# A decoder layer on one core: a new order of the opening stage, with block sums behind the shifts and one fold of squares

## The chip, the cores and the metric

One core of a Trainium2 chip runs one program. The metric is device time in microseconds (us) of one execution; the kernel before takes 1634.56 us as the median of 3 runs (1634.46 to 1636.76). Engines: PE (TensorE, matrix products), DVE (VectorE), ACT (ScalarE), POOL (GpSimd), SP (SyncE, which issues the loads).

## What is computed

A layer of a decoder on x of 1024 tokens by 1024 channels, in f32. Cut to the part that the change touches:

```python
mod = silu(cond) @ w_mod + b_mod                    # shifts, scales and gates
(sh1, sc1, g1, sh2, sc2, g2, sh3, sc3, g3) = split(mod, 9)
h = rms_norm(x, ffn1_norm) * (1 + sc1) + sh1
x = x + 0.5 * g1 * ((silu(h @ w_gate) * (h @ w_up)) @ w_down)
```

Behind this come a mixing layer (a short convolution beside a diagonal state-space model), a second feed-forward layer of the same form, and a last norm.

## The kernel before, in words

Tokens lie along the free axis in two halves of 512 (h = 0 and 1), channels on the 128 partitions in 8 blocks (k = 0 to 7). PE multiplies f32 values as pairs of a rounded high part and a rest: `mm3` (L342) makes each product of 128 by 128 by 512 from three matmuls, high by high, high by low, low by high. So every weight tile needs a rounding on ACT (`Weights.cast`, L173) and a subtraction on DVE (L177), and every block of activations a rounding (L980) and a subtraction (L984).

The opening stage (L845 to L1034) runs from the start until the first 64 products of the feed-forward layer are done: 2 halves, 8 blocks, 4 weight tiles of 128 output columns. Its instructions on PE, DVE, ACT and SP are written out by hand: `STEPS` (L1014) is a list of words, each word calls a function `do_...` with its digits, and the block `manual_schedule` (L1026) keeps that order on each of the four engines. Each engine works through its own queue in order. Instructions from outside the list can be placed between them by the scheduler. The words:

- `warm7`: 7 fillers (L926), matmuls of a bf16 tile of ones with itself, 512 columns, whose result nobody reads.
- `silu`, `cps0`, `cps1`, `cact`: silu of cond on one row, spread to 128 partitions by an f32 matmul with one row of weights for each 512 columns (L914), copied to SBUF (L918).
- `sqa12`, `sqd12`: the squares of the load of x with half 1 and pair of blocks 2, on ACT (L933) or on DVE (L937). `add12` folds the two blocks of a pair into one on DVE (L942). `stp12` adds a pair into the sum over all channels (L948): one f32 matmul of 512 columns if the pair was folded, two if not.
- `ya1`, `y1`: from the sum of half 1 the inverse root on ACT (L959, L960), and one step that sharpens it on DVE (L963, L964).
- `mods1`: for block 1 the two dot products with silu(cond) on DVE (L524; scale first, shift second) and two small instructions (L971, L972). The new words `ma1` and `mb1` are its two parts.
- `sc10`, `hi10`, `lo10` for block 1, half 0: scale (DVE, L976), shift and round (ACT, L980), shift and rest (DVE, L984).
- `wh0`, `wl0`: the rounding and the rest of weight tile 0. Tile 4, for the next stage, waits for a buffer that comes free when the products of tile 0 are done.
- `p111`: the product of half 1, block 1, weight tile 1.
- `x11`, `cols`, `half10`, `load3`, `rawh0`, `raw2`: loads issued by SP: a quarter of a half of x (512 KB), the table of small vectors (64 KB), half of a modulation block (512 KB), a whole one (1 MB), half of the first raw weight block, a whole one. There are four buffers for modulation blocks, and raw blocks 2 and 3 go where raw blocks 0 and 1 lay.
- `Weights.combine` (L154), the block sums: three passes of DVE (L157 to L159) over raw weight block 3 for the products of the next stage. It is called by `pump` (L184) and lies outside the list before; the new word `cmb3` calls it from the list.

```python
for c in range(2 - ((h, j) in added)):
    T.matmul(st[h][:], lhsT=means[D][:].to_broadcast([P, P]), rhs=sq[h, j][:, c, :], ...)
```

Of the kernel before, what the change touches and what calls it, by code (L numbers as in the profile page):

```python
# [13 lines left out]
F32 = mybir.dt.float32  # L14
# [7 lines left out]
P = 128  # L22
# [197 lines left out]
def hymba_layer(ctx: ExitStack, tc, x_d, wm1_d, wmod_d, gu1_d, gg1_d, gs1_d, wd1_d, win_d, wout_d, glu_d, gu2_d, gs2_d, wd2_d, cols_d, cond_d, lam_d, bc_d, out_d):  # L220
    nc = tc.nc
    V, A, T, SP = nc.vector, nc.scalar, nc.tensor, nc.sync

    def pool(name, bufs=1, **kw):
        return ctx.enter_context(tc.tile_pool(name=name, bufs=bufs, **kw))
# [11 lines left out]
    cact = pool("cap").tile([P, 1024], F32, name="cact")  # L237
# [22 lines left out]
    def t2k(name):  # L260
        return tmp.tile([P, HALF], F32, tag="t", name=name)

    cols = const.tile([P, NCOLS], F32, name="cols")
# [7 lines left out]
    gains = const.tile([P, C_CW - C_N1], F32, name="gains")  # L271
# [55 lines left out]
    ws = Weights((V, A, SP), srcs, granules, 2)  # L327
# [5 lines left out]
    def x_tile(k, h, nm):  # L333

        xt[k][h] = mov(f"{nm}{k}_{h}", dtype=F32)
        for i in range(2):
            x[2 * k + i][h] = xt[k][h][:, i, :]
        return xt[k][h][:]
# [183 lines left out]
    def mod_vector(w, s):  # L522

        V.tensor_tensor_reduce(out=w, in0=w, in1=cact[:], scale=1.0, scalar=0.0, op0=ALU.mult, op1=ALU.add, accum_out=s)  # L524
# [316 lines left out]
    pro = pro_open.enter_context(tc.tile_pool(name="pro", bufs=1))  # L841
# [10 lines left out]
    mw = {}  # L852

    def halves(t):

        return t.rearrange("p a c -> (p a c)").rearrange("(a p c) -> a p c", a=2, p=P)

    def mod_load(k, half=None):
        if k not in mw:
            mw[k] = pro.tile([P, 2, 1024], F32, tag="mw", name=f"mw{k}", bufs=4)  # L860
        if half is None:
            SP.dma_start(mw[k][:], wm1_d[k])
        else:
            SP.dma_start(mw[k][:, half, :], halves(wm1_d[k])[half])

    def raw_load(half):
        if not raw0:
            raw0.append(ws.blank())
        SP.dma_start(raw0[0][:, half, :], halves(gu1_d[0])[half])

    def x_load(h, j):
        SP.dma_start(x_tile(j, h, "x"), x_d[h, j])

    raw0 = []
    raw_load(0)
    x_load(1, 0)
    x_load(1, 2)
    x_load(1, 3)
    mod_load(1, 0)
    x_load(1, 1)  # L880
    SP.dma_start(cols[:], cols_d)
    mod_load(1, 1)
    mod_load(0, 0)
    mod_load(0, 1)
    x_load(0, 3)
    x_load(0, 1)
    x_load(0, 2)
    x_load(0, 0)
    raw_load(1)
    ws.load(2)  # L890
    mod_load(5)
    mod_load(2)
    b1 = cols[:, C_BMOD + SC1 * KT : C_BMOD + (SC1 + 1) * KT]
    cps = [ps(f"cp{i}") for i in range(2)]
    bcs = [pro.tile([P, HALF], F32, name=f"pbc{h}") for h in range(2)]
# [67 lines left out]
        V.scalar_tensor_tensor(out=y2[h], in0=st[h][:], scalar=EPS, in1=y2[h], op0=ALU.add, op1=ALU.mult)  # L963
        V.scalar_tensor_tensor(out=bcs[h][:], in0=y2[h], scalar=-3.0, in1=y[h], op0=ALU.add, op1=ALU.mult)  # L964

    def do_mods(k):
        m = pro.tile([P, 2], F32, tag="m", name=f"m{k}", bufs=2)
        for c in range(2):
            mod_vector(mw[k][:, c, :], m[:, c : c + 1])
        gn, sh = gains[:, k : k + 1], cols[:, C_BMOD + SH1 * KT + k : C_BMOD + SH1 * KT + k + 1]  # L970
        V.scalar_tensor_tensor(out=scl[:, 0, k : k + 1], in0=m[:, 0:1], scalar=gn, in1=pre[:, k : k + 1], op0=ALU.mult, op1=ALU.add)  # L971
        V.tensor_tensor(out=mods[:, 0, k : k + 1], in0=m[:, 1:2], in1=sh, op=ALU.add)  # L972
# [20 lines left out]
    def do_p(h, k, i):  # L993
# [4 lines left out]
        if i == 0 and made[0, 0] == made[1, 0] == KT:  # L998
            ws.slots.append(ringp)
            ws.freed += 1  # L1000

    def do_half(k, c):
        mod_load(k, c)

# [7 lines left out]
        ws.load(i + 1)  # L1012

    STEPS = """  # L1014
    warm7 warm7 warm1 silu wh0 ars wl0 sqd12 sqa10 cps0 cps1 sqa13 add12 add10 stp12 cact add13 stp10 sqa11 stp13 gains add11 mods1
    load3 warm3 stp11 ya1 mods0 sqa03 y1 sqa01 add03 sqa02 add01 warm7 warm7 warm7 warm2 stp03 sc11 sqa00 stp01 add02 hi11 add00
    stp02 wh1 sc01 stp00 lo11 hi01 p110 wl1 raw2 load7 ya0 p111 lo01 wh2 p101 y0 p100 wh3 sc10 wl2 hi10 warm7 p112 lo10 p102 sc00
    p010 wl3 hi00 p011 p113 lo00 p001 mods5 load6 raw3 p000 p013 p003 p002 sc51 p103 sc50 hi51 p012 hi50 lo51 p152 lo50 p052 mods2
    load4 p151 p153 p053 p050 sc21 p150 sc20 hi21 p051 hi20 lo21 p121 lo20 p020 mods6 p022 p120 p123 sc61 p023 sc60 p122 hi61 p021
    hi60 lo61 p162 lo60 p062 mods3 p161 p060 p163 sc30 p061 sc31 p160 hi30 p063 hi31 lo30 p033 lo31 p131 mods4 p132 p130 p030 sc41  # L1020
    p032 sc40 p133 hi41 p031 hi40 lo41 p141 lo40 p041 mods7 p040 p043 p042 sc71 p142 sc70 hi71 p140 hi70 p143 lo71 p170 lo70 p070
    p172 wh4 p071 wl4 p072 p171 p173 p073
    """
    todo = locals()
    ws.hold = True
    with tc.manual_schedule(engines={mybir.EngineType.DVE, mybir.EngineType.Activation, mybir.EngineType.PE, mybir.EngineType.SP}):  # L1026
        for step in STEPS.split():
            name = step.rstrip("01234567")
# [574 lines left out]
    f = t2k("u23f")  # L1603
# [12 lines left out]
    c = t2k("u23c")  # L1616
# [356 lines left out]
```

## Time and profile before

| | us |
|---|---|
| median of 3 runs | 1634.56 |
| the profiled execution | 1634.58 |
| its span | 1632.8 |
| PE busy in the span | 1618.8 (99%) |
| DVE busy | 1247.0 (76%) |
| ACT busy | 694.3 (43%) |
| first opening product on PE starts | 23.68 |
| first matmul of the next stage starts | 71.71 |

A row of a timeline holds the start, the time taken, the engine, the line, the operation, out<-in and how many were merged into the row; in square brackets the idle time of the engine before it and what ended it. PEld is PE's weight load, which precedes each matmul. The time of one matmul runs until its end is modelled to leave the array, so matmuls overlap; how far apart two of them start tells what one costs in a row of many. The same holds for DVE in a smaller measure.

### The profile page before, as it was taken

Reading aid. Unit: us, or ns where it says so; the run is one execution under the profiler, and the core shown is the slowest. Engines: PE = TensorE matmul, PEld = TensorE weight load, DVE = VectorE, ACT = ScalarE, POOL = GpSimd, SP = SyncE. Lnnn points to the kernel's source line nnn. Section 1 sums busy time; section 2 is a strip of 40 time slices with the busy share of each in tenths; the row PEclk is TensorE's granted clock in tenths of the full one; section 3 lists DMA queues with packets and bytes.
Section 4 is the critical chain, followed back from the end, with each engine's and each line's share of the span. In section 5 each row is a group of like instructions: output and inputs, shape, how many; then the busy total and the mean of one; then the engine's idle time right before and its main releaser. Section 6 shows DMA issues by size and latency. Waiting matters only on the chain.

```text
span 1632.8 us, 19772 instructions
## 1 busy us (share of the span) xinstructions
PE 1618.8 (99%) x7380; PEld 1328.6 (81%) x7380; DVE 1247.0 (76%) x1890; ACT 694.3 (43%) x949; POOL 2.0 (0%) x7
## 2 busy tenths in 40 slices
PE   9999999999999999999999999999999999999998
PEld 5788888888888888888887888888888888888887
DVE  8999888787778987888967968866676666557564
ACT  5354333333343435455546324433333333435351
POOL 0000000000000000000000000000000000000000
PEclk9999999999999999999999999999999999999999
DMA  9235565765688998434644642544554445668642
GB/s 380 89 105 174 192 217 187 250 223 194 217 306 332 330 331 292 148 84 148 232 136 162 228 146 104 173 175 155 187 197 168 166 169 180 222 238 284 226 136 104
DMA packets 149859, 325.99 MB, mean 200 GB/s; under 512 B 19585, under 2 KB 35201, under 8 KB 141826
## 3 DMA queue, kind: packets, MB, share of 16 engines
q1 hardware_dynamic: 149490, 324.46, 57.0%
q8 instruction: 58, 0.95, 0.2%
q14 instruction: 39, 0.32, 0.1%
q10 hardware_dynamic: 272, 0.26, 0.0%
HBM read 233.97 MB, written 90.70 MB: 199 GB/s over the span
## 4 chain that ended last, share of the span: by engine, by line
PE 87%; DVE 6%; issue 5%; ACT 1%; DMA 1%; SPq 0%; POOLq 0%; DVEq 0%; ACTq 0%
PE faDX L346 2%; PE faDX L347 2%; PE faDX L348 2%; PE faDY L346 2%; PE faDY L347 2%; PE faDY L348 2%; PE fbDX L346 2%; PE fbDX L348 2%; PE fbDX L347 2%; PE wo L346 1%; PE wo L348 1%; PE wo L347 1%; PE fbDY L346 1%; PE fbDY L348 1%; PE fbDY L347 1%
## 5 line engine op out<-in xcount | busy, mean ns | idle before, releaser
L177 DVE TENSOR_TENSOR w<-big,w 128x1024 fp32r<-128x1024 f32 x262 | 317.7, 1214 | 162.0 <-ACT w L173 161.7
L173 ACT CAST w<-big 128x1024 fp32r<-128x1024 f32 x262 | 272.9, 1045 | 235.5 <-issue 71.1
L524 DVE CUSTOM_DVE_ANT_0 wm<-wm,cact 128x1024 f32<-128x1024 f32 x56 | 68.4, 1222 | 18.8 <-DMA wm<-in_wmod 18.6
L347 PE MATMUL fbDX<-fbLl,w 128*128 128x512 f32 (+1 forms) x216 | 75.1, 348 | 0.0
L346 PE MATMUL fbDX<-fbLh,w 128*128 128x512 f32 (+1 forms) x216 | 74.9, 347 | 0.0
L348 PE MATMUL fbDX<-fbLh,w 128*128 128x512 f32 (+1 forms) x216 | 74.7, 346 | 0.0
L762 ACT CAST faLh<-faLr 128x1024 fp32r<-128x1024 f32 (+1 forms) x42 | 41.1, 980 | 65.4 <-DMA faLr<-l_d 60.3
L346 PE MATMUL faDX<-faLh,w 128*128 128x512 f32 x172 | 67.3, 391 | 0.0
L348 PE MATMUL faDX<-faLh,w 128*128 128x512 f32 x172 | 66.9, 389 | 0.0
L347 PE MATMUL faDX<-faLl,w 128*128 128x512 f32 x172 | 66.9, 389 | 0.0
L763 DVE TENSOR_TENSOR faLl<-faLr,faLh 128x1024 fp32r<-128x1024 f32 (+1 forms) x42 | 47.6, 1135 | 14.0 <-ACT faLh L762 14.0
L157 DVE TENSOR_TENSOR big<-big 128x1024 f32<-128x1024 f32 x46 | 56.1, 1220 | 2.2 <-DMA big<-in_gs 1.7
L763 DVE TENSOR_TENSOR fbLl<-fbLr,fbLh 128x1024 fp32r<-128x1024 f32 (+1 forms) x42 | 46.9, 1132 | 11.6 <-ACT fbLh L762 11.3
L346 PE MATMUL faDY<-faLh,w 128*128 128x512 f32 x132 | 51.3, 389 | 0.0
L347 PE MATMUL faDY<-faLl,w 128*128 128x512 f32 x132 | 51.3, 389 | 0.0
L348 PE MATMUL faDY<-faLh,w 128*128 128x512 f32 x132 | 51.3, 389 | 0.0
L346 PE MATMUL fbDY<-fbLh,w 128*128 128x512 f32 x132 | 51.3, 389 | 0.0
L347 PE MATMUL fbDY<-fbLl,w 128*128 128x512 f32 x132 | 51.3, 389 | 0.0
L348 PE MATMUL fbDY<-fbLh,w 128*128 128x512 f32 x132 | 51.3, 389 | 0.0
L762 ACT CAST fbLh<-fbLr 128x1024 fp32r<-128x1024 f32 (+1 forms) x42 | 40.4, 977 | 14.4 <-DMA fbLr<-l_d 13.4
L347 PEld LDWEIGHTS fbDX<-fbLl,w 128*128 128x128 f32 x216 | 40.9, 189 | 5.3 <-issue 0.2
L348 PEld LDWEIGHTS fbDX<-fbLh,w 128*128 128x128 f32 x216 | 40.9, 189 | 5.3 <-issue 0.2
(3189 smaller groups left out, 4456.4 us busy)
## 6 DMA issues: line engine op xcount, KB each, us to landing
big<-in_gs SPq DMA_DIRECT2D x39, 1024.0 KB, 5.2
wm<-in_wmod SPq DMA_DIRECT2D x56, 512.0 KB, 6.8
wd<-in_wd SPq DMA_DIRECT2D x44, 512.0 KB, 5.7
t_d<-wd SPq DMA_DIRECT2D x44, 512.0 KB, 3.6
faLr<-l_d SPq DMA_DIRECT2D x35, 512.0 KB, 7.9
fbLr<-l_d SPq DMA_DIRECT2D x35, 512.0 KB, 6.5
big<-t_d SPq DMA_DIRECT2D x16, 1024.0 KB, 5.7
big<-in_wd SPq DMA_DIRECT2D x12, 1024.0 KB, 6.1
```

Of the source, the lines that this page charges most:

```text
L157: self.V.tensor_tensor(out=big[:, 4:6, :], in0=big[:, r + 1 : r + 3, :], in1=big[:, r : r + 2, :], op=ALU.subtract)
L173: self.A.copy(top, src)
L177: self.V.tensor_tensor(out=rest, in0=src, in1=top.bitcast(F32), op=ALU.subtract)
L346: T.matmul(out, lhsT=hi, rhs=ah, start=first, stop=False, skip_group_check=more)
L347: T.matmul(out, lhsT=hi, rhs=al, start=False, stop=False, skip_group_check=more)
L348: T.matmul(out, lhsT=lo, rhs=ah, start=False, stop=last, skip_group_check=more)
L524: V.tensor_tensor_reduce(out=w, in0=w, in1=cact[:], scale=1.0, scalar=0.0, op0=ALU.mult, op1=ALU.add, accum_out=s)
L762: A.copy(hi[:, :c, :], src)
L763: V.tensor_tensor(out=lo[:, :c, :], in0=src, in1=hi[:, :c, :].bitcast(F32), op=ALU.subtract)
```

## The change

The loads that stood in program text ahead of the list move into the list, in another order. `mods` is split into `ma` and `mb`, and the list gets words for the table, for halves of raw weight block 0, and for the block sums. The list itself is new: 7 of 8 folds are gone, two of the squares move from ACT to DVE, the block sums stand near the end, and the numbers of fillers differ (7 + 7 + 6, 7 + 7 + 7 + 1, 1, 7 + 4, 7 + 2 and 7 + 5 + 7 + 3 ahead of the first product, none behind it).

```diff
--- before.py
+++ after.py
@@ -871,25 +871,7 @@
     def x_load(h, j):
         SP.dma_start(x_tile(j, h, "x"), x_d[h, j])
 
-    raw0 = []
-    raw_load(0)
-    x_load(1, 0)
-    x_load(1, 2)
-    x_load(1, 3)
-    mod_load(1, 0)
-    x_load(1, 1)
-    SP.dma_start(cols[:], cols_d)
-    mod_load(1, 1)
-    mod_load(0, 0)
-    mod_load(0, 1)
-    x_load(0, 3)
-    x_load(0, 1)
-    x_load(0, 2)
-    x_load(0, 0)
-    raw_load(1)
-    ws.load(2)
-    mod_load(5)
-    mod_load(2)
+    raw0, mv = [], {}
     b1 = cols[:, C_BMOD + SC1 * KT : C_BMOD + (SC1 + 1) * KT]
     cps = [ps(f"cp{i}") for i in range(2)]
     bcs = [pro.tile([P, HALF], F32, name=f"pbc{h}") for h in range(2)]
@@ -963,10 +945,13 @@
         V.scalar_tensor_tensor(out=y2[h], in0=st[h][:], scalar=EPS, in1=y2[h], op0=ALU.add, op1=ALU.mult)
         V.scalar_tensor_tensor(out=bcs[h][:], in0=y2[h], scalar=-3.0, in1=y[h], op0=ALU.add, op1=ALU.mult)
 
-    def do_mods(k):
-        m = pro.tile([P, 2], F32, tag="m", name=f"m{k}", bufs=2)
-        for c in range(2):
-            mod_vector(mw[k][:, c, :], m[:, c : c + 1])
+    def do_ma(k):
+        mv[k] = pro.tile([P, 2], F32, tag="m", name=f"m{k}", bufs=2)
+        mod_vector(mw[k][:, 0, :], mv[k][:, 0:1])
+
+    def do_mb(k):
+        m = mv[k]
+        mod_vector(mw[k][:, 1, :], m[:, 1:2])
         gn, sh = gains[:, k : k + 1], cols[:, C_BMOD + SH1 * KT + k : C_BMOD + SH1 * KT + k + 1]
         V.scalar_tensor_tensor(out=scl[:, 0, k : k + 1], in0=m[:, 0:1], scalar=gn, in1=pre[:, k : k + 1], op0=ALU.mult, op1=ALU.add)
         V.tensor_tensor(out=mods[:, 0, k : k + 1], in0=m[:, 1:2], in1=sh, op=ALU.add)
@@ -999,6 +984,15 @@
             ws.slots.append(ringp)
             ws.freed += 1
 
+    def do_cmb(j):
+        ws.combine(j)
+
+    def do_cols():
+        SP.dma_start(cols[:], cols_d)
+
+    def do_rawh(i):
+        raw_load(i)
+
     def do_half(k, c):
         mod_load(k, c)
 
@@ -1012,14 +1006,16 @@
         ws.load(i + 1)
 
     STEPS = """
-    warm7 warm7 warm1 silu wh0 ars wl0 sqd12 sqa10 cps0 cps1 sqa13 add12 add10 stp12 cact add13 stp10 sqa11 stp13 gains add11 mods1
-    load3 warm3 stp11 ya1 mods0 sqa03 y1 sqa01 add03 sqa02 add01 warm7 warm7 warm7 warm2 stp03 sc11 sqa00 stp01 add02 hi11 add00
-    stp02 wh1 sc01 stp00 lo11 hi01 p110 wl1 raw2 load7 ya0 p111 lo01 wh2 p101 y0 p100 wh3 sc10 wl2 hi10 warm7 p112 lo10 p102 sc00
-    p010 wl3 hi00 p011 p113 lo00 p001 mods5 load6 raw3 p000 p013 p003 p002 sc51 p103 sc50 hi51 p012 hi50 lo51 p152 lo50 p052 mods2
-    load4 p151 p153 p053 p050 sc21 p150 sc20 hi21 p051 hi20 lo21 p121 lo20 p020 mods6 p022 p120 p123 sc61 p023 sc60 p122 hi61 p021
-    hi60 lo61 p162 lo60 p062 mods3 p161 p060 p163 sc30 p061 sc31 p160 hi30 p063 hi31 lo30 p033 lo31 p131 mods4 p132 p130 p030 sc41
-    p032 sc40 p133 hi41 p031 hi40 lo41 p141 lo40 p041 mods7 p040 p043 p042 sc71 p142 sc70 hi71 p140 hi70 p143 lo71 p170 lo70 p070
-    p172 wh4 p071 wl4 p072 p171 p173 p073
+    silu x11 cols x12 x13 x10 half10 sqd12 ars warm7 warm7 warm6 cps1 sqd13 half11 x03 sqa11 cps0 rawh0 warm7 warm7 warm7
+    warm1 stp12 x01 warm1 stp13 x00 x02 gains half00 cact sqa10 ma1 stp11 mb1 stp10 ya1 y1 half01 sqa03 wh0 sc11 warm7
+    warm4 stp03 sqd01 hi11 add01 wl0 lo11 ma0 sqa00 mb0 sqa02 warm7 warm2 stp01 stp00 sc01 stp02 ya0 rawh1 raw1 wh1 hi01
+    wh2 y0 lo01 wl1 sc10 wh3 wl3 hi10 load5 warm7 warm5 warm7 warm3 p111 lo10 wl2 sc00 hi00 ma5 p110 lo00 p100 p113 load2
+    mb5 raw2 ma2 sc51 hi51 mb2 p011 lo51 sc50 raw3 p012 load6 hi50 sc21 load3 p013 p112 p103 sc20 p003 lo50 p002
+    p101 load4 load7 ma6 p000 p001 p102 p010 p151 p150 hi20 lo20 mb6 p153 hi21 lo21 sc61 hi61 p152 p052 ma3 p050
+    lo61 sc60 mb3 p051 p021 p020 hi60 lo60 p023 sc31 p122 sc30 p022 p120 p053 p161 ma4 hi30 p160 p162 p163 p060
+    p062 p121 hi31 lo30 p063 p061 p033 p123 lo31 p133 p130 mb4 p031 sc41 ma7 hi41 lo41 mb7 sc40 p032 sc70 p140
+    hi40 hi70 sc71 hi71 p030 p131 lo40 p143 p132 p142 p040 lo70 p070 lo71 p170 p043 p071 p072 wh4 p173 wl4 p041
+    p171 p172 p141 cmb3 p073 p042
     """
     todo = locals()
     ws.hold = True
```

## Rows read from the trace of the kernel before

**Rows 1.** Windows: length, busy (count) of PE, PEld, DVE, ACT, POOL, then clock, DMA, GB/s.
```profile
1.67:23.68 22.01, 21.36 (x61) 8.66 (x62) 15.61 (x29) 15.33 (x20) 0.00 (x0) 0.92 1.00 390
23.68:71.71 48.03, 47.10 (x202) 36.28 (x201) 47.35 (x82) 17.41 (x24) 0.00 (x0) 1.00 0.44 173
...
700.00:960.00 260.00, 256.39 (x1243) 212.59 (x1243) 212.67 (x334) 129.35 (x188) 0.00 (x0) 1.00 0.52 171
```

**Rows 2.** Timeline of PE, from the start to the first opening product.
```profile
1.67 5.64 PE L926 MATMUL warm<-busy 128*128 128x512 bf16 x15 [1.67 <-DVE busy L847]
7.24 1.98 PE L914 MATMUL cp<-cact,ones 1*128 1x512 f32 x4
...
15.61 5.13 PE L926 MATMUL warm<-busy 128*128 128x512 bf16 x23
20.58 3.67 PE L948 MATMUL pst<-xq,mean 128*128 128x512 f32 x8
23.68 0.80 PE L346 MATMUL p<-h,w 128*128 128x512 f32 x1
```

**Rows 3.** Timeline of weight loads: early fillers, and an f32 matmul of a sum.
```profile
2.50 0.15 PEld L926 LDWEIGHTS <-busy 128*128 128x128 bf16 x1 [0.28 <-issue]
2.92 0.15 PEld L926 LDWEIGHTS <-busy 128*128 128x128 bf16 x1 [0.28 <-issue]
...
21.01 0.19 PEld L948 LDWEIGHTS pst<-xq,mean 128*128 128x128 f32 x1 [0.24 <-DVE xq L942]
21.44 0.19 PEld L948 LDWEIGHTS pst<-xq,mean 128*128 128x128 f32 x1 [0.24 <-issue]
```

**Rows 4.** The tile of the opening products, and the timeline where they end.
```profile
L346 PE MATMUL p<-h,w x64: 388/389/799, 23.7 to 71.0; 128*128 128x512 f32 x64
...
71.03 0.39 PE L346 MATMUL p<-h,w 128*128 128x512 f32 x1
...
71.71 0.39 PE L346 MATMUL fa1g<-h,w 128*128 128x512 f32 x1
```

**Rows 5.** Timeline: squares that waited for the third and fourth load.
```profile
7.86 1.23 DVE L937 TENSOR_TENSOR xq<-x 128x1024 f32<-128x1024 f32 x1 [0.66 <-DMA x<-in_x]
...
9.11 1.06 ACT L933 ACTIVATE xq<-x 128x1024 f32<-128x1024 f32 x1 [0.71 <-DMA x<-in_x]
```

**Rows 6.** Timeline of DVE: block 0's sums, y1, folds, block 5, and block 2's start.
```profile
15.84 1.22 DVE L524 CUSTOM_DVE_ANT_0 mw<-mw,cact 128x1024 f32<-128x1024 f32 x1
...
18.33 0.69 DVE L963 SCALAR_TENSOR_TENSOR p1q<-pst,p1q 128x512 f32<-128x512 f32 x1
...
19.66 1.28 DVE L942 TENSOR_TENSOR xq<-xq 128x512 f32<-128x512 f32 x2
...
32.23 1.22 DVE L524 CUSTOM_DVE_ANT_0 mw<-mw,cact 128x1024 f32<-128x1024 f32 x1
...
33.37 1.22 DVE L524 CUSTOM_DVE_ANT_0 mw<-mw,cact 128x1024 f32<-128x1024 f32 x1
...
37.65 1.22 DVE L524 CUSTOM_DVE_ANT_0 mw<-mw,cact 128x1024 f32<-128x1024 f32 x1
```

**Rows 7.** Timeline of ACT around the root of half 1.
```profile
15.81 0.69 ACT L959 ACTIVATE p1y<-pst,eps 128x512 f32<-128x512 f32 x1 [3.11 <-PE pst L948]
...
17.07 1.04 ACT L933 ACTIVATE xq<-x 128x1024 f32<-128x1024 f32 x1
```

**Rows 8.** Windows of the opening, columns as in rows 1: the granted clock.
```profile
6.40:9.80 3.40, 2.82 (x9) 0.86 (x6) 2.71 (x4) 2.68 (x4) 0.00 (x0) 0.98 1.01 387
9.80:13.20 3.40, 3.33 (x4) 1.52 (x5) 2.03 (x6) 2.39 (x4) 0.00 (x0) 0.52 1.01 402
13.20:23.68 10.48, 10.48 (x39) 4.55 (x38) 10.45 (x22) 7.25 (x9) 0.00 (x0) 1.00 1.03 426
```

**Rows 9.** Timeline of DVE behind the last shifts: outside work and weight tile 4.
```profile
66.77 2.07 DVE L572 SCALAR_TENSOR_TENSOR x<-x,h1both,x 128x512 f32<-128x512 f32 x3
...
69.89 1.22 DVE L177 TENSOR_TENSOR w<-big,w 128x1024 fp32r<-128x1024 f32 x1
```

## Prediction

> **What bounds the kernel now.** I read the table of busy time by stretches first. TensorE (PE) is busy for almost the whole span, so a time won or lost before its first real product is kept unless a later stall takes it up. The table has three stretches that matter [rows 1]: up to 23.68 us PE holds only fillers, broadcasts and sums of squares; from 23.68 to 71.71 it works on the 64 opening products; and even in the stretch with the most stalls, 700 to 960 us, it is idle for only 260.00 - 256.39 = 3.6 us. VectorE (DVE) is busy for 47.35 of the 48.03 us of the products, so there the two are nearly level. What ends the opening is whichever of the two queues comes last, and both run in the order of the step list, one instruction after the other. So I add up each queue in the new order. The profiled execution took 1634.58 us (span 1632.8), 0.02 from the median of the runs shown, and the sum is made against it. A difference of 0.2%, 3.3 us, is about what a measurement can tell from none.
>
> **PE's prices.** The timeline of PE shows 15 fillers from 1.67 to 7.24 and 23 fillers from 15.61 to 20.58 [rows 2]. The second group gives (20.58 - 15.61) / 23 = 0.216 us each. The early ones are 0.42 to 0.43 apart [rows 3], so 11 at 0.43 and 4 at 0.216 make the first group. An f32 matmul of 512 columns stands in the trace as two rows, 0.43 apart at the full clock [rows 3]. An opening product is three matmuls, 71.71 - 71.03 = 0.68 us, and there are 64 [rows 4].
>
> A rule of the Trainium skill speaks against my price of a filler: TensorE: Matmul & The Clock Gate, section Back-to-back issue gap, gives about 131 ns as the sustained pace of weight load plus 512 columns, and 216 only for the isolated gap. By it the 74 fillers at full clock would cost 74 x 0.085 = 6.3 us less and the whole would come to 1638.3, still slower. The 23 fillers of this trace are such pairs, and their 0.216 decides against the 131.
>
> **Removed folds on PE.** A folded pair of squares needs one matmul (two rows, 0.86 us), an unfolded one two (four rows, 1.72 us). Before, all 8 are folded: 16 rows. Now 7 are not: 30 rows. That is 14 x 0.43 = +6.0 us of PE. **Fillers:** 48 before, 41 of them ahead of the first product; now 85, all ahead of it. Nothing hides either: PE is in order, and the first product stands behind them all.
>
> **PE's sum in the new order.** 20 fillers: 11 x 0.43 + 9 x 0.216, from 1.67 to 8.3. The two broadcasts, 4 x 0.43: 10.0. 23 fillers (22 and one between two sums): the four unfolded sums of half 1, 16 x 0.43 = 6.9, end at 21.9 with these 23 x 0.216 = 5.0 counted in. 11 fillers: 24.3; stp03: 26.0; 9 fillers: 27.9; stp01, stp00, stp02 (2 + 4 + 4 rows): 32.2; 22 fillers: 36.9. Only then p111, where the first product began at 23.68. 64 x 0.68 = 43.6 more gives 80.5 with no wait at all. This is a lower bound, 8.8 us above 71.71.
>
> **Are the data late anyway?** No. Loads of 512 KB land 1.25 us apart, the third at 7.86 and the fourth at 9.11 [rows 5]. In the new order x12 is the second large load, x13 the third, x10 the fourth, the two halves of block 1's modulation the fifth and sixth: about 6.6, 8.1 (the small table stands between), 9.3, 10.6, 11.8. The square of x12 is done by 7.8 (a pass of 1024 costs DVE 1.14 [rows 6]), but PE reaches stp12 only at about 14.8, behind 42 fillers. They do not fill a wait; they make one.
>
> **DVE's sum.** In the trace ScalarE (ACT) forms the root 0.1 us behind the last sum and takes 17.07 - 15.81 = 1.26 us for it [rows 7]. So now: last sum 22.0, root 23.3. The two passes of y1 take 19.66 - 18.33 = 1.33 [rows 6]: 24.65. DVE had block 1's modulation at 13.3 and stands still until 23.3; everything is queued behind y1. Then sc11, sqd01, add01, wl0, lo11, ma0 and mb0, sc01: 0.67 + 1.14 + 0.61 + 1.14 + 0.67 + 2.5 + 0.67 = 7.4, to 32.05; a pass of 512 costs 0.61 to 0.67 and a block's two sums 18.33 - 15.84 = 2.5 [rows 6]. y0 needs the root of half 0, whose last sum ends at 32.3: root 33.6, y0 35.0. lo01 waits for ACT (behind the root a cast of 1024, some 1.0, and a rounding of 512, some 0.7, as the passes of [rows 7]): 36.0; wl1 37.1. Just in time for the third matmul of p111 at 37.3. Then sc10, wl3, lo10, wl2, sc00, lo00 = 5.0: 42.1. Six blocks are left; one costs 37.65 - 32.23 = 5.42 with its two modulation sums, two scalings and two shifts [rows 6], of which 0.2 is a wait for ACT that the interleaved order avoids. 6 x 5.42 = 32.5 gives 74.6, 6 x 5.2 gives 73.3. Behind the last shift PE has 11 products, 7.5 us: 80.8 to 82.1.
>
> So PE alone gives 80.5 and DVE 80.8 to 82.1. I take 81.7 for the first matmul after the opening, which stood at 71.71: **+10.0 us, 1634.58 + 10.0 = 1644.6.**
>
> **What DVE gains, and why it pays nothing.** Seven folds go (7 x 0.61 = 4.3 us), two squares come from ACT (sqd13 and sqd01, 2 x 1.14 = 2.3), and the block sums (estimate 1.14 + 2 x 0.61 = 2.4, by the passes in [rows 6]) go behind the last shift. Some 4.4 us less lie ahead of that shift, against an idle wait of 10 at y1. The block sums behind wl4 are covered: they cost PE nothing while 5 products are left and the next weight is not yet due; without that cover they would cost 2.4.
>
> **Loads.** SyncE now holds raw2 until wl1 (37.1) and raw3 until wl2 and wl3 (41), and behind them stand loads 6, 3, 4 and 7. At 2.5 us a MB and some 2 for the way, load 6 lands at 47 to 49. DVE asks for it at about 52, so it costs nothing; were it later, DVE would wait as long. Loads 3, 4, 7 follow at 2.5 and are asked for at 5 to 6.
>
> **What the trace can't price.** *The clock.* Between 9.80 and 13.20 the granted clock was 0.52, that is 1.2 GHz, after a stretch in which PE had 0.6 us of idle time and the broadcasts with one row of weights; then 1.00 [rows 8]. In the new order PE never idles there and has 9 fillers and most of the broadcasts in that stretch. A second fall costs half of 3.4, 1.7 us; none costs 0, and an earlier first rise would win at most as much. I take 0, as the stretches that follow have it. The Trainium skill (same page, Part 1) has the clock throttled by default and released by activity; by that rule a PE without idle time keeps it, and the 0 stands. The trace agrees from 13.20 on, and cannot show the new stretch. *Work from outside the list* (x prepared for the next stage, 69.89 - 66.77 = 3.1 us in one block before wl4 [rows 9]) may be placed ahead of the last shifts or behind them: 0 to 3.1; I take 0, where it stood.
>
> **Rivals.**
> 1. *Fillers cost nothing* (the other side, not slower). If PE reached the end of stp10 by 12 instead of 21.9, y1 could run at 13.3, when block 1's modulation is there: 14.6, +7.4 = 22.0, y0, lo01 and wl1 25.2, +5.0 +32.5 = 62.7, + 7.5 = 70.2. That is 1.5 below 71.71: 1633.1, no change. Even the order's ideal is hardly a gain, as 64 products behind 25.2 end at 68.8 and DVE's total is near the old one. For it: the data are early. Against: the pitch of [rows 2]. It decides where the pitch of a filler falls well below 0.1. Chance 0.08 (0.02 of it faster by over 3.3 us).
> 2. *The clock falls once more*: 1646.3. For it: it did before [rows 8]. Chance 0.18.
> 3. *Outside work ahead of the last shifts*: up to 3.1, 1647.7. Against: in the trace it stood behind. Chance 0.08.
> 4. *Stalls later on take up part.* All 3.6 us of 700 to 960 [rows 1] would give 1641.0. Against: each of these follows a product of its own stage and moves with it, and DVE leaves the opening as late as PE. Chance 0.06.
>
> **The numbers.** The forecast has 0.60, by itself 1643.4 (PE's bound) to 1645.5. The range 1641.0 to 1649.5 takes in rival 4 below and 2 and 3 together above, and leaves out rival 1. Faster 0.02, same 0.06, slower 0.92.
>
> **What would show it.** Right: fillers still at 0.216; first sum of squares on PE near 15, first product near 37; DVE idle for some 10 us ahead of y1, released by ACT, and ACT in turn by PE; 30 rows of sums; 64 products with little wait; the next stage's first matmul near 82 and every later stage as much later. Wrong: a first product before 30, or a later stretch whose PE idle time shrinks by microseconds, would make the step from opening to total false; a first product near 37 with the next stage at 76 would mean that the products run faster than 0.68.

## The result, and the profile after

The changed kernel takes **1643.84 us** (median of 6 runs, 1642.81 to 1644.66); the kernel before, run beside it, 1634.51 (6 runs, 1633.57 to 1636.76). The ratio is 1.0056, 95% interval [1.0043, 1.0068]: 9.3 us slower, where 10.0 slower was forecast. The profiled executions have spans of 1642.1 and 1632.8 us. Beside the last experiment below, two of 15 runs of the kernel before took 2324.68 and 2732.89 us at a granted clock of 0.653 and 0.555; its ratio goes without them.

The windows of the kernel after, columns as in [rows 1]. The first line is the time up to the first opening product (it ends 0.2 us behind that product's start), the second the 64 products with the first of the next stage, the third the stretch that answers to 700 to 960 of before, the last two the clock at the start:

```profile
1.67:37.05 35.38, 35.37 (x120) 15.07 (x120) 17.25 (x28) 16.40 (x22) 0.00 (x0) 1.00 0.75 299
37.05:81.70 44.65, 44.64 (x196) 36.25 (x195) 44.65 (x81) 15.07 (x23) 0.00 (x0) 1.00 0.36 141
710.00:970.00 260.00, 256.44 (x1244) 212.70 (x1243) 212.65 (x335) 129.27 (x188) 0.00 (x0) 1.00 0.52 171
...
5.50:9.80 4.30, 4.30 (x16) 1.63 (x14) 2.10 (x2) 0.31 (x1) 0.00 (x0) 1.00 0.93 348
9.80:13.20 3.40, 3.40 (x17) 1.57 (x17) 2.21 (x6) 2.03 (x3) 0.00 (x0) 1.00 1.02 419
```

PE is without a gap for 35.37 of 35.38 us and yet starts its first product 13.2 us later than in [rows 2]. DVE, busy for 15.61 of 22.01 us before [rows 1], is now busy for 17.25 of 35.38. So the early stretch is PE's own, and what PE does there is the question. The timeline of PE after:

```profile
1.67 6.35 PE L908 MATMUL warm<-busy 128*128 128x512 bf16 x20 [1.67 <-DVE busy L847]
7.95 1.98 PE L896 MATMUL cp<-cact,ones 1*128 1x512 f32 x4
9.86 4.92 PE L908 MATMUL warm<-busy 128*128 128x512 bf16 x22
14.62 1.88 PE L930 MATMUL pst<-xq,mean 128*128 128x512 f32 x4
16.34 0.38 PE L908 MATMUL warm<-busy 128*128 128x512 bf16 x1
16.55 5.31 PE L930 MATMUL pst<-xq,mean 128*128 128x512 f32 x12
21.70 2.54 PE L908 MATMUL warm<-busy 128*128 128x512 bf16 x11
24.25 1.98 PE L930 MATMUL pst<-xq,mean 128*128 128x512 f32 x4
26.07 2.11 PE L908 MATMUL warm<-busy 128*128 128x512 bf16 x9
28.02 4.45 PE L930 MATMUL pst<-xq,mean 128*128 128x512 f32 x10
32.31 4.91 PE L908 MATMUL warm<-busy 128*128 128x512 bf16 x22
36.87 0.58 PE L346 MATMUL p<-h,w 128*128 128x512 f32 x1
...
81.20 0.39 PE L346 MATMUL fa1g<-h,w 128*128 128x512 f32 x1
```

Fillers and sums alternate, and no row behind the first shows idle time. 22 fillers take 14.62 - 9.86 = 4.76 us, 0.216 each (from here on, the pitch); 30 rows of sums stand where 16 stood. The next stage begins at 81.20 instead of 71.71 [rows 4]: 9.49 later, and the span is 9.3 longer. Of the 13.2 us at the first product, 3.7 thus come back in the products, which take 81.20 - 36.87 = 44.33 us instead of 48.03 [rows 1]. PE's timeline before shows why:

```profile
27.25 1.68 PE L926 MATMUL warm<-busy 128*128 128x512 bf16 x7
28.59 0.58 PE L346 MATMUL p<-h,w 128*128 128x512 f32 x1
...
49.42 0.50 PE L347 MATMUL p<-h,w 128*128 128x512 f32 x1 [0.66 <-DVE h L984]
```

Seven fillers stood among the products before, 28.59 - 27.25 = 1.3 us, and all fillers stand ahead of them now; the other 2.4 us were waits, most of them for DVE, which now has its lead. Behind the opening next to nothing comes back: 710 to 970 holds 260.00 - 256.44 = 3.56 us of idle PE, 3.61 before [rows 1].

The timelines of ACT and of DVE after show who waits for whom:

```profile
21.91 0.69 ACT L941 ACTIVATE p1y<-pst,eps 128x512 f32<-128x512 f32 x1 [9.85 <-PE pst L930]
```

```profile
23.29 0.69 DVE L945 SCALAR_TENSOR_TENSOR p1q<-pst,p1q 128x512 f32<-128x512 f32 x1 [9.10 <-ACT p1q L942]
...
33.89 0.69 DVE L945 SCALAR_TENSOR_TENSOR p0q<-pst,p0q 128x512 f32<-128x512 f32 x1 [1.53 <-ACT p0q L942]
...
41.52 1.21 DVE L524 CUSTOM_DVE_ANT_0 mw<-mw,cact 128x1024 f32<-128x1024 f32 x1
...
71.10 2.07 DVE L969 SCALAR_TENSOR_TENSOR h<-x,mods,h 128x512 fp32r<-128x512 f32 x3
73.08 0.16 DVE L565 TENSOR_TENSOR h1both<-mods 128x4 f32<-128x4 f32 x1
...
73.28 2.08 DVE L572 SCALAR_TENSOR_TENSOR x<-x,h1both,x 128x512 f32<-128x512 f32 x3
...
77.07 1.22 DVE L177 TENSOR_TENSOR w<-big,w 128x1024 fp32r<-128x1024 f32 x1
78.21 1.22 DVE L157 TENSOR_TENSOR big<-big 128x1024 f32<-128x1024 f32 x1
```

Read the brackets backwards: y1 on DVE waited 9.10 us for ACT's root, and ACT had waited 9.85 us for PE's last sum, which stood behind 43 fillers. The block sums (from L157 on) now stand behind the last shift, which ends at 73.08, where the next row starts.

### The profile page after: what moved, and what is told of

Read it like the earlier page. It is cut to its first block, busy times and chain, and to the rows that moved or that the text cites. A ratio compares the mean times of both kernels' runs of the same rounds, so it can differ in the third digit from the quotient of the medians.

```text
span 1642.1 us, 19873 instructions
## 1 busy us (share of the span) xinstructions
PE 1629.7 (99%) x7431; PEld 1334.6 (81%) x7431; DVE 1244.2 (76%) x1885; ACT 691.0 (42%) x947; POOL 2.0 (0%) x7
## 4 chain that ended last, share of the span: by engine, by line
PE 90%; issue 5%; DVE 3%; ACT 1%; DMA 1%; POOLq 0%; SPq 0%; DVEq 0%; ACTq 0%
PE faDX L347 2%; PE faDX L346 2%; PE faDX L348 2%; PE faDY L347 2%; PE faDY L346 2%; PE faDY L348 2%; PE fbDX L348 2%; PE fbDX L346 2%; PE fbDX L347 2%; PE wo L346 1%; PE wo L348 1%; PE wo L347 1%; PE warm L908 1%; PE fbDY L348 1%; PE fbDY L346 1%
## 5 line engine op out<-in xcount | busy, mean ns | idle before, releaser
L524 DVE CUSTOM_DVE_ANT_0 wm<-wm,cact 128x1024 f32<-128x1024 f32 x56 | 68.3, 1221 | 23.3 <-DMA wm<-in_wmod 23.1
L157 DVE TENSOR_TENSOR big<-big 128x1024 f32<-128x1024 f32 x46 | 56.1, 1220 | 2.1 <-DMA big<-in_gs 1.6
```

Source lines behind the costliest of these rows:

```text
L157: self.V.tensor_tensor(out=big[:, 4:6, :], in0=big[:, r + 1 : r + 3, :], in1=big[:, r : r + 2, :], op=ALU.subtract)
```

## Experiments

Each experiment edits the list of steps alone (one adds the step that places the block sums), and none changes what the layer computes. Ratios are to the kernel before, run on the same chip. Its median there was 1634.67 for the runs with 44 more fillers, without the 65 fillers, with one fold and with the block sums alone, 1634.63 for the last one and 1634.66 for the other four. Differences between two changed kernels are taken between such runs, some of them on two different chips. "Next stage" is the start of the first matmul behind the opening products, 71.71 before and 81.20 after.

**44 more fillers in the kernel before.** The price of a filler where its data are ready, by itself.

```diff
-add01 warm7 warm7 warm7 warm2 stp03
+add01 warm7 warm7 warm7 warm2 warm7 warm7 warm7 warm7 warm7 warm7 warm2 stp03
```

> The kernel before with 44 more fillers ahead of stp03, so that 85 stand ahead of the first product as in the changed one. My theory: 44 x 0.216 = 9.5 us more on PE ahead of the sums of half 0, first product at 33, y0 and all of DVE behind it as much later, next stage at 80.7 instead of 71.7: 1643.6 us. Rival (fillers stand in time in which PE would wait anyway, and the new loads or the unfolded sums make the loss): 1634.5, no change.

Measured: 1643.95 us, ratio 1.0057 [1.0043, 1.0071], so +9.3. PE's timeline:

```profile
17.68 14.62 PE L926 MATMUL warm<-busy 128*128 128x512 bf16 x67
32.14 3.60 PE L948 MATMUL pst<-xq,mean 128*128 128x512 f32 x8
...
82.99 0.39 PE L346 MATMUL fa1g<-h,w 128*128 128x512 f32 x1
```

67 fillers take 32.14 - 17.68 = 14.46 us, 0.216 each; 44 of them are 9.5, and the time grew by 9.3. This profiled execution (1645.0) is one of the two longest of five (1642.06 to 1645.18): its fillers begin 2.1 us later than in [rows 2], as the clock stayed low for longer there (last section), and its next stage comes 82.99 - 71.71 = 11.3 us later. So a filler put where PE's data are ready is on the path at its full price, and there the rival that fillers cost nothing is false.

**The changed kernel without the 65 fillers behind the broadcasts.**

```diff
-cps0 rawh0 warm7 warm7 warm7 warm1 stp12 x01 warm1 stp13 ... sc11 warm7 warm4 stp03 ... sqa02 warm7 warm2 stp01 ... load5 warm7 warm5 warm7 warm3 p111
+cps0 rawh0 stp12 x01 stp13 ... sc11 stp03 ... sqa02 stp01 ... load5 p111
```

> The changed kernel without the 65 fillers that stand between the broadcasts and the first product (the first 20 stay). My theory (PE's queue, and DVE behind it, sets the opening): PE reaches the last sum of half 1 at about 16.5 instead of 21.9, y1 starts at 18 instead of 23.3, the first product at 29 instead of 36.9; then DVE binds and the next stage starts at 75.6, 5.6 us earlier than the changed kernel: 1638.2 us, or 1.7 to 3.4 more where the clock falls in PE's new idle time. Rival (fillers stand in time in which PE would wait anyway): no change, 1643.8.

Measured: 1640.17 us, ratio 1.0036 [1.0023, 1.0048]. That is 3.7 less than the changed kernel, for 65 x 0.216 = 14.0 us of fillers. PE's and DVE's timelines, then windows around the first products, columns as in [rows 1]:

```profile
29.13 0.50 PE L346 MATMUL p<-h,w 128*128 128x512 f32 x1 [2.37 <-ACT w L173]
...
76.49 0.39 PE L346 MATMUL fa1g<-h,w 128*128 128x512 f32 x1
```

```profile
18.08 0.69 DVE L945 SCALAR_TENSOR_TENSOR p1q<-pst,p1q 128x512 f32<-128x512 f32 x1 [3.64 <-ACT p1q L942]
```

```profile
29.10:32.10 3.00, 1.15 (x4) 0.67 (x5) 2.86 (x4) 2.49 (x3) 0.00 (x0) 1.00 0.05 22
32.10:35.50 3.40, 3.40 (x10) 2.62 (x9) 3.40 (x5) 0.72 (x1) 0.00 (x0) 0.50 0.81 284
```

y1 starts 5.2 us earlier than in the kernel after and waits 3.64 us instead of 9.10. Of the 5.2, 0.3 was there at the broadcasts (7.62 against 7.95), and the rest is what the 23 fillers ahead of it cost. The first product starts only 7.7 earlier, though 42 more fillers, 9.1 us, are gone ahead of it. Then PE is short of data (busy for 1.15 of 3.00 us), and from 32.10 to 35.50 the granted clock is 0.50, that is 1.2 GHz. The products take 76.49 - 29.13 = 47.4 us against 44.3, and the next stage starts at 76.49. So the fillers cost what stands in front of ready data; most of the 42 had filled waits that are there without them, and had kept the clock. This profiled execution (1638.88) is the shortest of five. This kernel is still 5.5 us slower than before with fewer fillers than it, so fillers are not all of the loss.

**24 of the 65 put back** where the trace of the last run shows PE waiting.

```diff
-sc11 stp03 ... sqa02 stp01 ... load5 p111
+sc11 warm7 warm3 stp03 ... sqa02 warm4 stp01 ... load5 warm7 warm3 p111
```

> The changed kernel with 24 fillers in place of the 65 behind the broadcasts, only where the kernel without them had PE idle: 10 ahead of stp03, 4 ahead of stp01, 10 ahead of the first product. My theory: fillers that stand in a true wait cost nothing and keep the clock at 2.4 GHz, so the fall to half that cost the kernel without them some 0.9 to 1.7 us is gone: 1638.5 to 1639.3 us, next stage at 75.6. Rival (each filler costs its 0.216 wherever it stands): 24 x 0.216 = 5.2 us more than the kernel without them, 1645.

Measured: 1639.48 us, ratio 1.0028 [1.0017, 1.0039]. PE's timeline and a window:

```profile
27.02 2.32 PE L908 MATMUL warm<-busy 128*128 128x512 bf16 x10
...
32.11 0.50 PE L348 MATMUL p<-h,w 128*128 128x512 f32 x1 [1.82 <-DVE w L177]
...
76.91 0.39 PE L346 MATMUL fa1g<-h,w 128*128 128x512 f32 x1
```

```profile
32.00:36.00 4.00, 3.89 (x11) 3.08 (x12) 4.00 (x6) 0.74 (x2) 0.00 (x0) 0.62 0.72 242
```

24 fillers, 5.2 us by the pitch, went in, and the time did not grow (0.7 less, with overlapping runs: 1638.66 to 1640.2 against 1638.88 to 1642.04). The next stage at 76.91 is 0.4 later than in the last run's trace, but so are the broadcasts, ahead of all fillers in question (8.05 against 7.62). In a true wait fillers are free. The clock I had expected to keep fell all the same: the wait that matters, 1.82 us for DVE's weight tile 1, lies inside the first product, behind the last fillers, where none of this list can cover it. Three of the five runs without the 24 have a mean granted clock of 0.995, and none of the seven with them is below 0.997, so some of the clock may be kept in other executions; that is not shown by a profile.

**The kernel before with one fold left** (add01), as in the change.

```diff
-sqa13 add12 add10 stp12 cact add13 stp10 sqa11 stp13 gains add11 mods1 ... sqa01 add03 sqa02 add01 ... stp01 add02 hi11 add00 stp02
+sqa13 stp12 cact stp10 sqa11 stp13 gains mods1 ... sqa01 sqa02 add01 ... stp01 hi11 stp02
```

> The kernel before with one fold of squares left (add01), all else as it was. My theory: 14 more rows of 0.43 us, 6.0 us, on PE ahead of the first product, which starts at 29 instead of 23.7; DVE's 4.3 us less don't help, as it waits for the sums; next stage at 77: 1640.0 us. Rival (DVE sets the opening, the fold's removal is its gain): 4.3 us less on DVE, 1630.2.

Measured: 1639.1 us, ratio 1.0026 [1.0017, 1.0035], so +4.4. PE's timeline:

```profile
21.87 6.17 PE L948 MATMUL pst<-xq,mean 128*128 128x512 f32 x14
27.48 0.80 PE L346 MATMUL p<-h,w 128*128 128x512 f32 x1
...
75.30 0.39 PE L346 MATMUL fa1g<-h,w 128*128 128x512 f32 x1
```

14 more rows of sums last 14 x 0.43 = 6.0 us, and the median run is 4.4 longer: most of the price is paid, and the 4.3 us that DVE no longer spends on folds don't make up for it. This profiled execution is one of the shortest (1637.5 of 1637.09 to 1640.11). In it the first product comes 3.8 us later than in [rows 2] and the next stage 3.6 later, and the clock does not fall early as it did in [rows 8]; at 0.52 the stretch from 9.80 to 13.20 would hold 1.6 us less work, and 3.8 + 1.6 = 5.4 is near the 6.0. The longer runs have no profile, but their mean clock is on record: the five runs at 0.997 took 1639.58 to 1640.11, the six at 0.998 or 0.999 took 1637.09 to 1639.1. A stretch such as 9.80 to 13.20 at half the clock lowers the mean over 1636 us by 0.001, so the longer runs fit one more such stretch; where it lies in them is not shown.

**The kernel before without its 33 later fillers.** The other side of the filler's price.

```diff
-mods1 load3 warm3 stp11 ... add01 warm7 warm7 warm7 warm2 stp03 ... hi10 warm7 p112
+mods1 load3 stp11 ... add01 stp03 ... hi10 p112
```

> The kernel before without the 33 fillers behind the broadcasts. My theory: they stand in waits of PE (for squares and folds), so taking them out frees no time: at the clock of before 1634.5 us; but PE now idles some 5 us ahead of the sums of half 0, and if the granted clock falls there the first products run at half pace for 3.4 us and it is slower by 1 to 2 us, 1636. Rival (each filler costs its 0.216 wherever it stands): 7.1 us less, 1627.5.

Measured: 1636.51 us, ratio 1.0011 [1.0002, 1.002]: 1.9 slower. PE's timeline of this kernel, a weight load of the kernel before at the same sum, then a window of this kernel:

```profile
20.39 6.23 PE L948 MATMUL pst<-xq,mean 128*128 128x512 f32 x8 [5.79 <-DVE xq L942]
```

```profile
20.40 0.37 PEld L948 LDWEIGHTS pst<-xq,mean 128*128 128x128 f32 x2 [0.15 <-DVE xq L942]
```

```profile
20.00:24.00 4.00, 3.60 (x5) 1.54 (x6) 4.00 (x7) 3.63 (x5) 0.00 (x0) 0.50 1.04 435
```

The kernel before had its 23 fillers in a wait: DVE's fold releases PE at 20.39 without them and at 20.40 with them. Without them PE stands still for 5.79 us, the clock falls to 0.50 and the sums take 6.23 us instead of 3.67 [rows 2]. All 11 runs have a mean clock of 0.994 to 0.996, the kernel before beside them 0.996 to 0.998. So the fillers of before were worth 1.9 us; those of the change stand elsewhere.

**The block sums alone:** the kernel before, with the sums of weight block 3 ahead of the last product.

```diff
+    def do_cmb(j):
+        ws.combine(j)
...
-p171 p173 p073
+p171 p173 cmb3 p073
```

> The kernel before with the block sums fixed behind weight tile 4, all else as it was. My theory: three passes of DVE, 2.4 us, leave the way to the last shifts, on which PE waits there; the last products end 2.0 us earlier: 1632.5 us. Rival (their place between the shifts is covered by products that PE still has): no change, 1634.5.

Measured: **1632.78 us**, ratio 0.9987 [0.9978, 0.9996], 1.9 less than the kernel before and the fastest of all that ran. Its timelines, DVE first, then PE:

```profile
69.29 1.22 DVE L157 TENSOR_TENSOR big<-big 128x1024 f32<-128x1024 f32 x1
```

```profile
23.96 0.80 PE L346 MATMUL p<-h,w 128*128 128x512 f32 x1
...
70.03 0.39 PE L346 MATMUL fa1g<-h,w 128*128 128x512 f32 x1
```

The first product is 0.3 later than in [rows 2], the next stage starts 1.7 earlier. Where PE waits for DVE among the products, as in the kernel before, taking 2.4 us of passes off DVE ahead of the last shift pays 1.9 of them.

**The changed kernel without that step** (the last lines read `p141 p073 p042`, without `cmb3`).

> The changed kernel with the block sums taken out of the list again, so that they lie where the scheduler puts them: the pass of 1024 ahead of the scalings of blocks 3 and 4, the two short ones behind the last shift. My theory (behind the wait at y1, DVE is level with PE, so what is put ahead of the last shifts moves the end): 1.1 us later, 1644.9 us. Rival (PE alone sets the opening of the changed kernel, DVE has room): no change, 1643.8.

Measured: 1644.32 us, ratio 1.0057 [1.0045, 1.007]; the changed kernel has 1.0056. By the times alone this is undecided. PE's timeline:

```profile
69.16 0.50 PE L347 MATMUL p<-h,w 128*128 128x512 f32 x1 [0.31 <-DVE h L969]
...
82.00 0.39 PE L346 MATMUL fa1g<-h,w 128*128 128x512 f32 x1
```

In the trace the sums stand at 65.42, 74.42 and 76.35, and the next stage starts at 82.00, 0.8 later, of which 0.18 was there at the first product. The other 0.6 are one wait of PE for a shift that stands behind the pass at 65.42: PE's starts up to 69.50 lie 0.70 and 0.34 us apart there, where 0.23 is usual. The changed kernel has no such wait. So in these two profiles the step that is worth 1.9 us in the kernel before is worth some 0.6, in an order in which DVE idles for 9 us ahead of the products and PE has no gap.

**The changed kernel with the first 18 loads in their old order** (12 of them leave their later places in the list).

```diff
-silu x11 cols x12 x13 x10 half10 sqd12 ...
+silu rawh0 x10 x12 x13 half10 x11 cols half11 half00 half01 x03 x01 x02 x00 rawh1 raw1 load5 load2 sqd12 ...
```

> The changed kernel with the first 18 loads in the order of the kernel before. My theory: every load still lands before PE or DVE comes to it, y1 waits for the sums and not for data: no change, 1643.8 us within 1. Rival (the new order of the loads makes part of the loss): up to several us less.

Measured: 1643.55 us, ratio 1.0053 [1.0041, 1.0066]. DVE's timeline:

```profile
22.76 0.69 DVE L945 SCALAR_TENSOR_TENSOR p1q<-pst,p1q 128x512 f32<-128x512 f32 x1 [6.50 <-ACT p1q L942]
```

DVE has its data later (it idles 6.50 us instead of 9.10), and y1 still waits for PE's sums. It starts 0.5 earlier than in the kernel after, as the broadcasts do (7.43 against 7.95). The order of these loads has no part in the result that the times show.

**The parts that cost, mended:** the changed kernel with 16 later fillers for 65, half 1 folded again, one square moved from DVE to ACT (its entry sqd01 becomes sqa01, earlier), and weight tile 1 and the first products reordered so that PE has work in the waits.

```diff
-cps0 rawh0 warm7 warm7 warm7 warm1 stp12 x01 warm1 stp13 ... sqa10 ma1 stp11 mb1 stp10
+cps0 rawh0 add12 stp12 x01 add13 stp13 ... sqa10 ma1 add11 stp11 mb1 add10 stp10
...
-mb0 sqa02 warm7 warm2 stp01 stp00 sc01 stp02 ya0 rawh1 raw1 wh1 hi01 wh2 y0 lo01 wl1 sc10
+mb0 sqa02 stp01 stp00 sc01 stp02 p110 warm6 rawh1 raw1 wh1 wl1 ya0 hi01 wh2 y0 lo01 p100 sc10
```

> The changed kernel without 65 of its fillers (16 put where PE waits), the four pairs of half 1 folded again, the square of x01 back on ACT, weight tile 1 split ahead of y0 and not behind it, and tile 0's products of blocks 1 and 0 first; loads, block sums and all products from block 5 on as in the changed kernel. My theory (what the kernel without the 65 fillers still lost against before came from the unfolded sums of half 1, 3.4 us on PE ahead of y1, and from weight tile 1 standing behind y0 on DVE): next stage at 72.9 instead of 76.5, 1635.9 us, or 1 to 2 more if the granted clock falls. Rival (the rest of the loss lies in the order of the later products and loads): no change against the kernel without fillers, 1640.2.

Measured: 1636.49 us, ratio 1.001 [1.0001, 1.0019]. PE's and DVE's lines:

```profile
25.50 0.80 PE L346 MATMUL p<-h,w 128*128 128x512 f32 x1
...
73.39 0.39 PE L346 MATMUL fa1g<-h,w 128*128 128x512 f32 x1
```

```profile
17.94 0.69 DVE L945 SCALAR_TENSOR_TENSOR p1q<-pst,p1q 128x512 f32<-128x512 f32 x1 [2.60 <-ACT p1q L942]
```

Of the 9.3 us lost 9.3 - 1.9 = 7.4 come back with these parts together; the share of each was not tried. Everything else of the new order is still in place. The 1.9 left stand at the first product already (25.50 against 23.68), and which of the remaining moves holds them was not tried. This kernel keeps the block sums behind the last shift; against the kernel before with that step alone (1632.78) it is still 3.7 slower.

## Why the prediction was right, point by point

- **The bound.** PE's queue set the opening, as the sum said. First sum 14.62 (14.8 forecast), last sum of half 1 ended 21.9 (21.9), stp03 ended 26.07 (26.0), the sums 32.31 (32.2), first product 36.87 (36.9). Both prices, 0.216 a filler and 0.43 a row of sums, held; the runs with 44 more fillers and with one fold priced each by itself.
- **The filler rule.** The changed kernel's 22 fillers at 0.216 us apart again do not agree with about 131 ns (the Trainium skill, TensorE: Matmul & The Clock Gate, section Back-to-back issue gap), nor do the 67 of the run with 44 more; the measurement decides. Rival 1, that fillers cost nothing, falls where the data are ready and holds in a true wait, as the runs with 24 put back and without the 33 in the kernel before show.
- **What fillers hide.** "Nothing hides either" is true of the 23 between the broadcasts and the last sum of half 1, and of PE's queue as it stands. It is not what the fillers cost: without 65 of them, 14.0 us, the kernel is 3.7 faster, as behind y1 DVE and ACT are nearly as late as PE.
- **DVE.** y1 at 23.29 (23.3), idle 9.10 ahead of it (some 10), y0 at 33.89 (33.6). The six blocks began at 41.52, with one shift of 0.66 of block 0 between their passes, so they took 73.08 - 42.18 = 30.9 us, 5.15 each, where I took 5.2 to 5.42. This is the mis-sized term: the last shift ended at 73.08, just below 73.3 to 74.6, and with 7.5 us of products behind it DVE would have allowed 80.6. So DVE did not come last, as the 81.7 had it; PE did. The 64 products took 44.33 for 43.6, and the waits that make up the 0.7 us beyond it stand at their start and before 50, not at the end. That 81.7 came near 81.20, +10.0 for +9.5, is in part luck: a DVE term too large stood in for waits that the sum did not have. The 1645.5 at the end of the main case does not follow from the sum either: 82.1 gives 1645.0.
- **Loads.** Load 6 landed at 48.9 (47 to 49) and was asked for at 51.1 (52). Nothing waited for it.
- **The clock** (rival 2). It was 1.00 from 5.50 on, earlier than the forecast needed (the broadcasts began at 7.95, not 8.3), and there was no second fall in this execution. The price of such a fall showed in the experiments instead.
- **Outside work** (rival 3) stood at 73.28, behind the last shifts and ahead of weight tile 4 at 77.07, as I took it. The block sums hid behind it.
- **Later stalls** (rival 4) took up nothing: 3.56 us of idle PE against 3.61.
- **What I had not separated.** The block sums alone are worth 1.9 us. The forecast had them as DVE time that pays nothing, which is nearly right in this order (some 0.6 us by the trace) and wrong in the kernel before.

## What to carry to other kernels

Warm-up matmuls sit in an in-order queue: put them only where a trace of the same order shows the engine waiting, for ahead of ready data each costs its full pitch, and in a wait they cost nothing and can save the clock. Work moved from an engine that waits to the one that it waits for (a fold on DVE traded for a matmul on PE) costs most of what it lasts there, here 4.4 of 6.0 us, whatever the other engine gains. Run the parts of a bundled change one by one: a step worth 1.9 us by itself stood here inside a loss of 9.3, in an order where it paid 0.6 at most by the trace.

## What the runs showed of the hardware that was not expected

The early clock differs between kernels whose first instructions are the same or nearly so. In the stretch 9.80 to 13.20 it was 0.52 before [rows 8], but these are the windows of the kernel before with 44 more fillers (two lines) and with one fold (one line):

```profile
9.80:13.20 3.40, 2.68 (x3) 1.18 (x4) 2.22 (x5) 2.67 (x4) 0.00 (x0) 0.50 1.02 407
13.20:16.50 3.30, 3.30 (x6) 1.13 (x5) 2.87 (x4) 0.40 (x1) 0.00 (x0) 0.50 1.03 422
```

```profile
9.80:13.20 3.40, 3.40 (x9) 1.52 (x8) 1.10 (x3) 2.58 (x4) 0.00 (x0) 1.00 1.03 407
```

In the first the low level lasts some 6.7 us, though its added fillers lie behind that stretch; in the second, whose list differs from before by the folds alone, it doesn't come. One stretch such as this at the low level or the full one is worth 1.6 to 1.7 us of work, so where PE is the bound two kernels that differ by that little are told apart by repeated runs and not by one profile. Where PE stood still for 5.79 us, or was busy for 1.15 of 3.00, the low level followed each time; the Trainium skill (TensorE: Matmul & The Clock Gate, Part 1: The HAM clock gate) has idleness bring the throttle back, and these two rows agree. The fall in [rows 8] came behind 0.6 us of idle time only.
